# State-space outputs with the states as weights, and the mixer's branches in the other order, in a hybrid decoder block

## The chip, the core and the metric

The kernel runs on one core of a Trainium2 chip. The metric is the device time of one execution in microseconds (us), as the median over runs. TensorE (PE) multiplies; its weight loads are listed apart as PEld. VectorE (DVE), ScalarE (ACT) and GpSimd (POOL) work element by element, and SyncE (SP) issues most of the DMA transfers.

## The reference

One layer of a decoder block over 512 tokens of width 2048, in float32. What matters here is the first half, the mixer:

```python
h = modulate(rmsnorm(x, g_mix), shift1, scale1)          # shift, scale, gate: silu(c) @ w_ada
proj = h @ w_in + b_in                                   # -> q 1024, k 256, v 256, u 1024, gates 2 x 2048
q, k = rope_partial(q), rope_partial(k)
y_attn = sliding_window_attention(q, k, v, sinks) @ w_attn_branch       # window 128, 16 heads of 64
y_ssm = s5_ssm(u, ...) @ w_ssm_branch                    # 64 groups of 16 channels, 64 complex states each
merged = g[:, :, 0] * y_attn + g[:, :, 1] * y_ssm        # g = sigmoid(gate logits)
x = x + gate1 * (merged @ w_out)
# then the second half: x + gate2 * peer(h2, ...), a retrieval over 16384 experts, and a last rmsnorm
```

The state-space branch (`s5_ssm`) is linear in u: a recurrence x[t] = a x[t-1] + B u[t] with complex diagonal a, and y = Re(C x) + D u. Then z = gelu(y), and z * sigmoid(z @ w_glu + b_glu) is its output.

## The kernel before

Every matrix product with weights from memory is made exact enough by splitting: `weights` loads a tile of 1024 weights a row (`raw`), ACT rounds it to `whi` (L186), DVE forms the rest `wlo` (L188), and three matmuls per 128 x 128 block (L202, L203, L204) multiply the high and low parts of weights and activations. One such matmul is called dense below. A projection of 128 columns of `w_in` is 48 dense matmuls on 512 columns. The kernel is written in order, and a scheduler decides when it is built how the instructions of each engine follow one another; on the chip each engine takes its own in that fixed order and waits where an operand or a buffer is not there yet.

The mixer has these stages:

- **Head.** The columns of h become ready in five cuts (`HEAD_CUTS`), since each needs its part of `w_ada`, which DVE multiplies out (L141). `head_product` (L440 to L442) multiplies each cut with the u columns of `w_in` and accumulates eight PSUM tiles. In cuts 1 and 2, POOL makes `wlo` in place of DVE. Meanwhile POOL builds the constants of the recurrence; the largest are the rotations `rc` and `rs`, powers of a unit complex number for 64 chunks, made by six doublings (`cmul`, L343 to L348). They are written to memory as `rot_d` (L530, issued by SP). u goes to memory too (`u_d`).
- **State space with projections between.** The 512 steps are 64 chunks of 8. `ssm_slice` treats 4 pairs of groups; there are 8 slices. In a slice, (A) POOL multiplies out the matrices into and out of the chunks' states (`mt`, `cl_r`, `cl_i`); (B) PE turns `mt` (L582) and forms the kernel inside a chunk (`km`, L591, L592), which goes through memory (`km_d`, L599) and comes back spread out as `iraw` (L601), and u is loaded chunk by chunk (`uc`) and permuted (L614); (C) PE forms the inputs of the states (L624), and DVE rotates them, scans over the chunks and rotates back (L630 to L653), which gives the states `x_r`, `x_i`; (D) PE forms y: 24 matmuls, with `cl_r`, `cl_i` or `intra` as weights of 128 columns and the states or u as 64 moving columns (L662 to L664). y goes to `y_d` in pieces of 256 bytes. Buffers of a slice are mostly single. Between the parts of a slice stand projections, first k, v and q (with rotary embedding, `rope`), then gate logits (`sg_d`).
- **Attention with projections between.** 16 blocks (`attend`, a key-value head by 128 queries): scores (L700), softmax on DVE, ACT and POOL, transposes (L722), times v (L727). Between a block's scores and its transposes stands one projection. Then come 12 more projections.
- **Branch products.** y is loaded, passed through gelu (L763) and split, and then come `w_ab`, `w_glu`, `w_sb` and `w_out` with dense matmuls.

The second half (the retrieval) takes the rest and is the same in both kernels.

Of the kernel before, what the change touches and what calls it, by code (L numbers as in the profile page):

```python
# [19 lines left out]
T = 512  # L20
TT = 4
# [39 lines left out]
def hybrid_block(tc, I, out, dbg=None):  # L61
# [118 lines left out]
    loads = []  # L180

    def split_weights(src, part, sub=tt):
        r = wts.tile([128, 8, 128], F32, name="raw", tag="raw", bufs=4)[:, 0:part]
        loads.append(nc.sync.dma_start(r.rearrange("p a b -> p (a b)"), src).ins)
        h = wts.tile([128, 8, 128], F32R, name="whi", tag="whi")[:, 0:part]
        nc.scalar.copy(h, r)  # L186
        l = wts.tile([128, 8, 128], F32R, name="wlo", tag="wlo")[:, 0:part]
        sub(l, r, h.bitcast(F32), op=OP.subtract)  # L188
        return h, l
# [183 lines left out]
    nc.gpsimd.memset(rc[:, :, 0:1], 1.0)  # L373
    nc.gpsimd.memset(rs[:, :, 0:1], 0.0)
    w = 1
    while w < 64:
        ub, vb = (z[:, :, None].to_broadcast([128, PAIRS, w]) for z in (ur, ui))
        cmul(rc[:, :, w:2 * w], rs[:, :, w:2 * w], rc[:, :, 0:w], rs[:, :, 0:w], ub, vb, ra[:, :, 0:w])
        cmul(vr, vi, ur, ui, ur, ui, t0)
        ur, ui, vr, vi = vr, vi, ur, ui  # L380
        w *= 2
# [49 lines left out]
    def head_product(c):  # L431
# [27 lines left out]
    y_d = dr.tile([1024, 8, 64], F32, name="y_d")  # L459
# [8 lines left out]

    ap_ = pool("ap", "left")
    qr = ap_.tile([128, 8, T], F32, name="qr")  # L470
    kr = ap_.tile([128, 2, T], F32, name="kr")
    vv = ap_.tile([128, TT, 256], F32, name="vv")
    rp = pool("rp", "left")
    rcos = rp.tile([128, T], F32, name="rcos")
    rsin = rp.tile([128, T], F32, name="rsin")
    posi = tmp.tile([128, T], I32, name="t0", tag="t0")
    ang = row("ev")
    nc.sync.dma_start(posi, I["positions"][None, :].to_broadcast([128, T]))
    nc.vector.tensor_copy(ang, posi)
    ts(ang, ang, freq, None, op0=OP.mult)  # L480
    reduce_angle(ang, rcos)
    sin_cos(rsin, rcos, ang)
    ts(rsin, rsin, sgn, None, op0=OP.mult)
# [22 lines left out]
    def dense():  # L506
        jobs = [(8 + i, rope, kr[:, i]) for i in range(2)]
        jobs += [(10 + i, value, vv[:, :, i * 128:(i + 1) * 128]) for i in range(2)]
        jobs += [(i, rope, qr[:, i]) for i in range(8)]
        last = None  # L510
        for m, finish, dst in jobs:
            o = projected(m)
            if last:
                last[0](*last[1:])
            last = finish, dst, o
            yield
        for i in range(32):
            o = projected(20 + i, 1)
            nc.scalar.dma_start(sg_d[i], o)
            if last:  # L520
                last[0](*last[1:])
                last = None
            yield

    dense_work = dense()
# [10 lines left out]
    with tc.issue_after(loads[-1]):  # L536
        nc.sync.dma_start(bass.AP(tensor=km_d.tensor, offset=km_d[0].offset + 128, ap=[[240, 128], [30720, 8], [1, 112]]),
                            zero[:, None, :].to_broadcast([128, 8, 112]))
# [7 lines left out]
    def ssm_slice(s):  # L546
# [21 lines left out]
        cl_r, cl_i = tl("cl_r", [128, 4, 16, 8]), tl("cl_i", [128, 4, 16, 8])  # L568
# [9 lines left out]
        for mt, name in zip(mts, ("mi_r", "mi_i")):  # L578
            dst = tl(name, [128, 4, 128])
# [20 lines left out]
        iraw, intra = tl("iraw", [128, 8, 128]), tl("intra", [128, 8, 16, 8])  # L600
# [3 lines left out]
        rot = tl("rot", [128, 2, 256])  # L604
# [6 lines left out]
        u = tl("uc", [128, 8, 64])  # L611
# [3 lines left out]
        uj = tl("uj", [128, 8, 64])  # L615
# [12 lines left out]
        ta = tl("t2", [128, 512])[:, 0:256]  # L628
        w_r, w_i = (tl("mt", [128, 4, 16, 8], 2).rearrange("p a h j -> p (a h j)")[:, 0:256] for _ in range(2))
# [11 lines left out]
        x_r, x_i = tl("x_r", [128, 4, 64]), tl("x_i", [128, 4, 64])  # L641
# [25 lines left out]

    slices = [ssm_slice(s) for s in range(8)]
    next(slices[0])
    for s in range(8):  # L670
        for _ in slices[s]:
            next(dense_work)
        if s < 7:
            next(slices[s + 1])
    close(ss)
    close(sp)
    close(rp)
# [11 lines left out]
    def attend(b, n):  # L689
# [7 lines left out]
        for r2 in range(2):  # L697
            p = aux_tile().rearrange("p (a c) -> p a c", a=2)
            for r in range(2):
                nc.tensor.matmul(p[:, r, 0:wd], qr[rows, np_ * 4 + r2 * 2 + r, b * 128:(b + 1) * 128],  # L700
                                 kr[rows, np_, k0:k0 + wd], start=True, stop=True)
# [13 lines left out]
        yield  # L715
# [3 lines left out]
        for kc in range(nk):  # L719
# [3 lines left out]
            pt = aw.tile([128, 512], F32, name="pt", tag="pt", bufs=3)  # L723
# [7 lines left out]
    for b in range(TT):  # L731
        for n in range(4):
            for _ in attend(b, n):
                next(dense_work)
    close(aw)
    close(ap_)
# [23 lines left out]
    for k in range(8):  # L760
        y = row("ev")
        nc.sync.dma_start(y, y_d[k * 128:(k + 1) * 128].rearrange("p j c -> p (j c)"))
        act(z[:, k].rearrange("p (c j) -> p c j", j=8), y.rearrange("p (j c) -> p c j", j=8)[:, :, ::-1], AF.Gelu_apprx_tanh)  # L763
# [480 lines left out]

def shape_constants():
# [17 lines left out]
def device_inputs(x):  # L1263
# [5 lines left out]
    b_in = np.concatenate([l["b_in"][:1024][qo], l["b_in"][1024:]])  # L1269
    d = {  # L1270
# [8 lines left out]
                                                     l["b_glu"])], axis=1),  # L1279
# [3 lines left out]
        "w_sb": chunked(l["w_ssm_branch"]),  # L1283
        "w_glu": chunked(l["w_glu"]),
# [33 lines left out]
```

## Time and profile before

| | |
|---|---|
| time, median of 3 runs | 3734.87 us (3728.91 to 3746.68) |
| the profiled execution's own time | 3761.78 us |
| its span, first to last instruction | 3760.0 us |
| granted TensorE clock, mean | 0.961 of full speed |
| busy: PE, DVE, ACT, POOL | 94%, 71%, 34%, 24% |
| head, to the last L442 | to 208.4 us |
| state space with projections | 212.2 to 557 us |
| attention with projections, rest of the projections | 557 to 929 us |

PE is busy nearly always, but a matmul counts as busy from its start to its modelled end, and these overlap; how long a matmul really takes its place is the distance to the start of the next one. POOL and DVE count only while they compute.

### The profile page before, as it was taken

Reading aid. Unit: us, or ns where it says so; the run is one execution under the profiler, and the core shown is the slowest. Engines: PE = TensorE matmul, PEld = TensorE weight load, DVE = VectorE, ACT = ScalarE, POOL = GpSimd, SP = SyncE. Lnnn points to the kernel's source line nnn. Section 1 sums busy time; section 2 is a strip of 40 time slices with the busy share of each in tenths; the row PEclk is TensorE's granted clock in tenths of the full one; section 3 lists DMA queues with packets and bytes.
Section 4 is the critical chain, followed back from the end, with each engine's and each line's share of the span. In section 5 each row is a group of like instructions: output and inputs, shape, how many; then the busy total and the mean of one; then the engine's idle time right before and its main releaser. Section 6 shows DMA issues by size and latency. Waiting matters only on the chain.

```text
span 3760.0 us, 51345 instructions
## 1 busy us (share of the span) xinstructions
PE 3551.0 (94%) x20045; PEld 3227.8 (86%) x20045; DVE 2686.4 (71%) x4037; ACT 1291.9 (34%) x1788; POOL 906.7 (24%) x818
## 2 busy tenths in 40 slices
PE   7699999999999988999699999999999999999997
PEld 3477777777788888999699999999999999999997
DVE  7643545556874359989787788888888888877844
ACT  3232223333543342267232332233323323333333
POOL 7744530010000145310121222121221222222102
PEclk8888989999999999999899999999999999999998
DMA  8642445446964322266998898999999899978833
GB/s 287 210 156 79 126 135 179 171 159 251 335 215 167 119 88 69 86 218 241 322 351 303 329 340 338 334 334 340 347 334 344 328 335 346 342 274 310 321 128 112
DMA packets 274104, 921.60 MB, mean 245 GB/s; under 512 B 35394, under 2 KB 92866, under 8 KB 229956
## 3 DMA queue, kind: packets, MB, share of 16 engines
q1 hardware_dynamic: 204260, 533.91, 40.3%
q0 software_dynamic: 50048, 344.55, 24.9%
q10 hardware_dynamic: 19552, 39.85, 2.8%
q8 instruction: 157, 2.57, 0.3%
q14 instruction: 87, 0.71, 0.1%
HBM read 871.03 MB, written 47.12 MB: 244 GB/s over the span
## 4 chain that ended last, share of the span: by engine, by line
PE 76%; DVE 8%; DMA 7%; issue 2%; ACT 1%; POOL 1%; SPq 0%; DVEq 0%; ACTq 0%; POOLq 0%
PE mm L204 15%; PE mm L202 15%; PE mm L203 15%; PE aux L1200 8%; PE aux L1199 8%; PE aux L1198 8%; DMA gt<-g_d 3%; DMA raw<-in_up 2%; DVE wlo L188 1%; PE aux L1111 1%; DMA iraw<-km_d 1%; PE aux L664 1%; ACT whi L186 1%; PE aux L700 1%; PE aux L727 1%
## 5 line engine op out<-in xcount | busy, mean ns | idle before, releaser
L186 ACT CAST whi<-raw 128x1024 fp32r<-128x1024 f32 (+2 forms) x744 | 759.8, 1022 | 1687.3 <-PE mm L203 761.0
L188 DVE TENSOR_TENSOR wlo<-raw,whi 128x1024 fp32r<-128x1024 f32 (+2 forms) x696 | 851.6, 1224 | 424.9 <-ACT whi L186 400.8
L204 PE MATMUL mm<-h_hi,wlo 128*128 128x352 f32 (+1 forms) x2752 | 952.0, 346 | 10.4 <-DVE wlo L188 10.2
L202 PE MATMUL mm<-h_hi,whi 128*128 128x352 f32 (+1 forms) x2752 | 950.6, 345 | 5.7 <-ACT whi L186 5.7
L203 PE MATMUL mm<-h_lo,whi 128*128 128x352 f32 (+1 forms) x2752 | 947.7, 344 | 0.0
L1198 PE MATMUL aux<-wh,whi 128*128 128x352 f32 x2048 | 671.0, 328 | 50.0 <-ACT wh L192 26.9
L1200 PE MATMUL aux<-wh,wlo 128*128 128x352 f32 x2048 | 673.6, 330 | 25.5 <-DVE wlo L188 25.4
L1199 PE MATMUL aux<-wl,whi 128*128 128x352 f32 x2048 | 670.5, 327 | 2.3 <-DVE wl L193 2.3
L204 PEld LDWEIGHTS mm<-h_hi,wlo 128*128 128x128 f32 x2752 | 523.6, 190 | 44.0 <-DVE wlo L188 14.2
L202 PEld LDWEIGHTS mm<-h_hi,whi 128*128 128x128 f32 x2752 | 523.2, 190 | 37.7 <-ACT whi L186 6.7
L203 PEld LDWEIGHTS mm<-h_lo,whi 128*128 128x128 f32 x2752 | 524.8, 191 | 32.0 <-issue 4.4
L1198 PEld LDWEIGHTS aux<-wh,whi 128*128 128x128 f32 x2048 | 393.3, 192 | 56.8 <-ACT whi L186 29.7
L1200 PEld LDWEIGHTS aux<-wh,wlo 128*128 128x128 f32 x2048 | 392.9, 192 | 33.0 <-DVE wlo L188 32.7
L1199 PEld LDWEIGHTS aux<-wl,whi 128*128 128x128 f32 x2048 | 392.8, 192 | 3.3 <-DVE wl L193 3.3
L1028 DVE SCALAR_TENSOR_TENSOR rows<-rows,hrow 128x2048 f32<-128x2048 f32 x160 | 365.4, 2284 | 17.2 <-DMA rows<-in_down_rows,pick 16.9
L141 DVE SCALAR_TENSOR_TENSOR adaw<-adaw,cb 128x1024 f32<-128x1024 f32 x176 | 230.5, 1316 | 146.9 <-DMA adaw<-in_w_ada 146.7
L1022 POOL DMA_INDIRECT rows<-in_down_rows,pick x128 | 149.8, 1170 | 693.3 <-DVE rows L1028 390.3
L1039 DVE SCALAR_TENSOR_TENSOR yrow<-rows,fit,yrow 128x2048 f32<-128x2048 f32 x127 | 297.9, 2346 | 0.1
L1022 POOL DMA_INDIRECT rows<-in_up_rows,pick x128 | 146.0, 1140 | 560.1 <-DVE rows L1028 446.9
L1201 DVE SCALAR_TENSOR_TENSOR x<-aux,mod,x 128x352 f32<-128x352 f32 x256 | 148.4, 580 | 140.1 <-PE aux L1200 139.7
L214 POOL TENSOR_TENSOR rstd<-rstd,t 128x512 f32<-128x512 f32 (+2 forms) x42 | 52.8, 1258 | 610.9 <-ACT t L212 610.2
L188 POOL TENSOR_TENSOR wlo<-raw,whi 128x1024 fp32r<-128x1024 f32 (+1 forms) x48 | 104.7, 2188 | 101.1 <-ACT whi L186 99.8
(439 smaller groups left out, 4529.0 us busy)
## 6 DMA issues: line engine op xcount, KB each, us to landing
raw<-in_down SPq DMA_DIRECT2D x256, 512.0 KB
raw<-in_up SPq DMA_DIRECT2D x256, 512.0 KB
adaw<-in_w_ada SPq DMA_DIRECT2D x192, 512.0 KB
raw<-in_w_in SPq DMA_DIRECT2D x88, 512.0 KB
g_d<-stg ACTq DMA_DIRECT2D x22, 1024.0 KB
gt<-g_d SPq DMA_DIRECT2D x16, 1408.0 KB
raw<-in_w_out SPq DMA_DIRECT2D x32, 512.0 KB
raw<-in_w_query SPq DMA_DIRECT2D x32, 512.0 KB
```

The costliest lines, as they stand in the source:

```text
L141: stt(w, w, 1.0, cb[:, half], op0=OP.mult, op1=OP.mult, accum_out=part[:, half:half + 1])
L186: nc.scalar.copy(h, r)
L188: sub(l, r, h.bitcast(F32), op=OP.subtract)
L202: nc.tensor.matmul(p, h[:, k], (xh[kk] if isinstance(xh, list) else xh[:, kk]), start=first, stop=False)
L203: nc.tensor.matmul(p, h[:, k], (xl[kk] if isinstance(xl, list) else xl[:, kk]), start=False, stop=False)
L204: nc.tensor.matmul(p, l[:, k], (xh[kk] if isinstance(xh, list) else xh[:, kk]), start=False, stop=last)
L1022: nc.gpsimd.indirect_dma_start(out=r.rearrange("p k c -> p (k c)"), out_offset=None, in_=I[table], in_offset=bass.IndirectOffsetOnAxis(ap= ...
L1028: stt(r, r, 1.0, hrow, op0=OP.mult, op1=OP.mult, accum_out=f[:, n:n + 1])
L1039: stt(y, r, f[:, n:n + 1], y, op0=OP.mult, op1=OP.add)
L1198: nc.tensor.matmul(p, h[:, j], WH[j], start=(j == 0), stop=False)
L1199: nc.tensor.matmul(p, h[:, j], WL[j], start=False, stop=False)
L1200: nc.tensor.matmul(p, l[:, j], WH[j], start=False, stop=(j == GI - 1))
```

## The change

It has six parts. (1) The rotations are built by a function, `rotations`, that is called after the last POOL `wlo` of the head, and `rot_d` and the zeros in `km_d` are written from POOL's queue. (2) The state space comes directly after the head, with 16 gate logits between, and k, v, q come after it. (3) In `ssm_slice` most buffers are double, DVE's work has buffers of its own (`ta`, `w_r`, `w_i`), and the parts of neighbouring slices are written interleaved, so that part A runs two slices ahead. (4) y is formed with the states (or u) as weights of 64 columns and `cl_r`, `cl_i` or `intra` as 128 moving columns, and then turned by 16 matmuls of 64 x 64; the gelu is taken there (L651), and the result goes to memory in whole rows. The channels of the state-space branch have another order for that (`state_order`, on the host). (5) In the attention the scores of a block are formed before the projections that precede the transposes of the block before. All projections are used up there: 7 of the 12 for k, v and q stand ahead of it, and the other 5 and 16 gate logits inside. (6) z is loaded with the gelu already taken.

```diff
-    nc.gpsimd.memset(rc[:, :, 0:1], 1.0)
...
+    def rotations(ur, ui, vr, vi):
+        nc.gpsimd.memset(rc[:, :, 0:1], 1.0)
+        nc.gpsimd.memset(rs[:, :, 0:1], 0.0)
+        w = 1
+        while w < 64:
+            ub, vb = (z[:, :, None].to_broadcast([128, PAIRS, w]) for z in (ur, ui))
+            cmul(rc[:, :, w:2 * w], rs[:, :, w:2 * w], rc[:, :, 0:w], rs[:, :, 0:w], ub, vb, ra[:, :, 0:w])
+            cmul(vr, vi, ur, ui, ur, ui, t0)
+            ur, ui, vr, vi = vr, vi, ur, ui
+            w *= 2
+        for i, t_ in enumerate((rc, rs)):
+            nc.gpsimd.dma_start(rot_d[:, :, i], t_.rearrange("p (a b) c -> p a b c", a=8))
...
+            if c == 2 and i == 7:
+
+                with tc.issue_after(subs[-1]):
+                    rotations(ur, ui, vr, vi)
...
-    with tc.issue_after(loads[-1]):
-        for i, t_ in enumerate((rc, rs)):
-            nc.sync.dma_start(rot_d[:, :, i], t_.rearrange("p (a b) c -> p a b c", a=8))
...
+        p = aux_tile()
+        for a in range(4):
+            for n_ in range(3):
+                for two in range(2):
+                    rows = slice(two * 64, two * 64 + 64)
+                    o = p[rows, a * 128:(a + 1) * 128]
+                    if n_ < 2:
+                        x_, cl_ = ((x_r, cl_r), (x_i, cl_i))[n_]
+                        nc.tensor.matmul(o, x_[rows, a], cl_[rows, a].rearrange("p h j -> p (h j)"), start=(n_ == 0), stop=False)
+                    else:
+                        nc.tensor.matmul(o, uj[:, 2 * a + two], intra[:, 4 * two + a].rearrange("p h j -> p (h j)"),
+                                         start=False, stop=True)
+        y = tl("y", [128, 8, 64])
+        nc.scalar.copy(y, p.rearrange("p (m j) -> p j m", j=8))
+        p = aux_tile()
+        for j in range(8):
+            for two in range(2):
+                rows = slice(two * 64, two * 64 + 64)
+                nc.tensor.matmul(p[rows, j * 64:(j + 1) * 64], y[rows, j], ident[rows, rows], start=True, stop=True)
+        zs = tl("zs", [128, T])
+        act(zs.rearrange("p (c j) -> p c j", j=8), p.rearrange("p (j c) -> p c j", j=8)[:, :, ::-1], AF.Gelu_apprx_tanh)
+        nc.scalar.dma_start(y_d[s], zs)
...
+    for s in range(8):
+        next(slices[s])
+        next(dense_work)
+        if s < 7:
+            next(slices[s + 1])
+        next(slices[s], None)
+        if s < 6:
+            next(slices[s + 2])
+        next(dense_work)
...
-        y = tl("uc", [128, 8, 64])
-        for two in range(2):
-            p = aux_tile()
-            rows = slice(two * 64, two * 64 + 64)
-            for a in range(4):
-                g = 2 * a + two
-                o = p[:, a * 64:(a + 1) * 64]
-                nc.tensor.matmul(o, cl_r[rows, a].rearrange("p h j -> p (h j)"), x_r[rows, a], start=True, stop=False)
-                nc.tensor.matmul(o, cl_i[rows, a].rearrange("p h j -> p (h j)"), x_i[rows, a], start=False, stop=False)
-                nc.tensor.matmul(o, intra[:, 4 * two + a].rearrange("p h j -> p (h j)"), uj[:, g], start=False, stop=True)
-            nc.scalar.copy(y[:, two::2], p[:, 0:256].rearrange("p (a c) -> p a c", a=4))
-        nc.scalar.dma_start(chunked_ap(y_d), y)
...
+    blocks = [attend(b, n) for n in range(4) for b in range(TT)]
+    next(blocks[0])
+    for i, block in enumerate(blocks):
+        with tc.issue_after(next(blocks[i + 1])) if i + 1 < len(blocks) else contextlib.nullcontext():
+            for _ in range(2 if i < 5 else 1):
+                next(dense_work, None)
+        next(block, None)
```

The order of POOL's instructions at the end of the head, before the change (L343 to L348 are the rotations, L188 is `wlo` of the head's weights, L544 the first instruction that uses the memory which `rc` and `rs` had):

```order
L346 TENSOR_TENSOR rs<-rc,sn 128x32x32
L344 TENSOR_TENSOR pt_135<-sn 128x32
L346 TENSOR_TENSOR vi<-cs,sn 128x32
L345 TENSOR_TENSOR rc<-rc,ra 128x32x32
L188 TENSOR_TENSOR wlo<-raw,whi 128x512
L345 TENSOR_TENSOR vr<-vr,pt_135 128x32
L188 TENSOR_TENSOR wlo<-raw,whi 128x512
L347 TENSOR_TENSOR ra<-rs,cs 128x1024
L188 TENSOR_TENSOR wlo<-raw,whi 128x512 x13
L544 MEMSET bd_1533 128x128
```

The same place of POOL after the change (L375 and L376 begin the rotations, L385 writes them to memory):

```order
L348 TENSOR_TENSOR vi<-vi,pt_135 128x32
L188 TENSOR_TENSOR wlo<-raw,whi 128x512 x16
L375 MEMSET rc 128x32
L376 MEMSET rs 128x32
L343 TENSOR_TENSOR cs<-vr 128x32
...
L347 TENSOR_TENSOR ra<-rs,cs 128x1024
L385 DMA rot_d<-rc 1024x1x256
L348 TENSOR_TENSOR rs<-rs,ra 128x32x32
L385 DMA rot_d<-rs 1024x1x256
L520 MEMSET bd_1499 128x128
```

All 16 `wlo` now stand ahead of the rotations; between L343 and L347 here 68 more instructions of the rotations are left out, and the first use of their memory follows directly behind the second write.

PE's order where a slice forms y, before (slice 2, counted from 0; the 64 at the end are the moving columns):

```order
L662 MATMUL aux<-x_r,cl_r 128x64 x2
L202 MATMUL mm<-h_hi,whi 128x512
L203 MATMUL mm<-h_lo,whi 128x512
L204 MATMUL mm<-h_hi,wlo 128x512
...
L663 MATMUL aux<-x_i,cl_i 128x64
L664 MATMUL aux<-uj,intra 128x64
L662 MATMUL aux<-x_r,cl_r 128x64
...
L582 MATMUL aux<-cst,mt 128x128 x8
```

PE's order at the same place of a slice after the change (`y` is the copy of the first result; `cst` is the identity that turns it):

```order
L639 MATMUL aux<-cl_r,x_r 64x128 x2
L639 MATMUL aux<-cl_i,x_i 64x128 x2
L641 MATMUL aux<-intra,uj 64x128 x2
L203 MATMUL mm<-h_lo,whi 128x512
L204 MATMUL mm<-h_hi,wlo 128x512
...
L649 MATMUL aux<-cst,y 64x64 x16
L600 MATMUL aux<-uc,mi_r 64x64 x8
L600 MATMUL aux<-uc,mi_i 64x64 x8
L558 MATMUL aux<-cst,mt 128x128 x4
```

The two halves of the output rows are now formed in turn (x2), with 128 moving columns. Rows that repeat are left out. The 24 matmuls are followed by 22 dense ones, the 16 that turn, part C of the next slice and the `mt` of the slice after it. Up to the first of the 24 there are 274 dense matmuls of `w_in` (192 of them ahead of the first `mt`, L558, where there were 74), and then 273 from the first of the 24 of slice 0 to that of slice 5; before, each slice had some 90.

SP's order at the end of the head, before (the loads of 128x256 are the head's last weights, those of 128x1024 the first dense ones):

```order
L184 DMA raw<-in_w_in 128x256 x12
L530 DMA rot_d<-rc 1024x1x256
L184 DMA raw<-in_w_in 128x1024
L530 DMA rot_d<-rs 1024x1x256
L537 DMA km_d<-t_1528 128x8x112
L184 DMA raw<-in_w_in 128x1024 x23
```

The same place of SP after:

```order
L184 DMA raw<-in_w_in 128x256 x13
L184 DMA raw<-in_w_in 128x1024
L137 DMA adaw<-in_w_ada 128x1024
L184 DMA raw<-in_w_in 128x1024
L137 DMA adaw<-in_w_ada 128x1024
```

The writes of `rot_d` and of the zeros in `km_d` have left this queue, and every load of gate weights has one of `w_ada` behind it from the first on.

## Rows read from the trace of the kernel before

**Rows 1.** Windows: stretch, length, busy of PE PEld DVE ACT POOL, clock, DMA share, GB/s.

```profile
70.00:104.00 34.00, 28.55 (x100) 20.89 (x100) 31.72 (x58) 10.89 (x19) 33.77 (x44) 0.83 0.89 317
104.00:132.60 28.60, 0.36 (x2) 0.00 (x0) 7.05 (x13) 0.00 (x0) 28.60 (x37) 0.58 0.14 50
132.60:208.40 75.80, 70.39 (x284) 54.39 (x284) 52.91 (x80) 29.25 (x50) 29.64 (x20) 0.96 0.72 244
208.40:212.20 3.80, 1.48 (x5) 0.42 (x3) 1.23 (x1) 2.13 (x2) 0.00 (x0) 0.85 1.07 386
212.20:557.00 344.80, 338.81 (x1804) 268.23 (x1804) 161.92 (x288) 90.77 (x113) 170.23 (x186) 0.88 0.39 120
557.00:929.00 372.00, 372.00 (x1608) 284.55 (x1608) 208.66 (x329) 129.99 (x271) 31.05 (x16) 0.99 0.50 182
```

**Rows 2.** PE in order of time: start, us, what, [idle before <-releaser].

```profile
132.61 0.80 PE L442 MATMUL aux<-h_hi,wlo 128*128 128x512 f32 x1 [28.25 <-POOL wlo L188]
```

**Rows 3.** POOL in order of time, the head's end and the first slice.

```profile
69.68 0.24 POOL L343 TENSOR_TENSOR cs<-vr 128x32 f32<-128x32 f32 x1
...
74.51 1.33 POOL L343 TENSOR_TENSOR rc<-rc,vr 128x32 f32<-128x32 f32 x1
...
138.51 3.37 POOL L348 TENSOR_TENSOR rs<-rs,ra 128x1024 f32<-128x1024 f32 x1
...
179.71 2.17 POOL L188 TENSOR_TENSOR wlo<-raw,whi 128x512 fp32r<-128x512 f32 x1 [1.46 <-ACT whi L186]
213.36 0.35 POOL L544 MEMSET bd<- 128x128 f32 x2 [31.49 <-DMA rot_d<-rs]
...
224.12 1.35 POOL L566 TENSOR_TENSOR mt<-mt,t 128x512 f32<-128x512 f32 x1
```

**Rows 4.** Chain that ended last, 140 to 260 us: start, us, what.

```profile
149.78 0.23 PE aux L440
...
201.68 8.04 DMA raw<-in_w_in
...
245.19 7.35 DMA iraw<-km_d
```

**Rows 5.** PE in order of time, y of slice 4 (from 0) and behind it.

```profile
424.36 0.44 PE L662 MATMUL aux<-x_r,cl_r 64*128 64x64 f32 x4
...
427.04 0.43 PE L662 MATMUL aux<-x_r,cl_r 64*128 64x64 f32 x2
427.32 0.38 PE L663 MATMUL aux<-x_i,cl_i 64*128 64x64 f32 x2
427.63 0.43 PE L664 MATMUL aux<-uj,intra 128*128 128x64 f32 x2
427.99 0.43 PE L662 MATMUL aux<-x_r,cl_r 64*128 64x64 f32 x2
...
431.38 0.69 PE L662 MATMUL aux<-x_r,cl_r 64*128 64x64 f32 x2
...
433.04 0.69 PE L662 MATMUL aux<-x_r,cl_r 64*128 64x64 f32 x2
...
436.22 1.91 PE L582 MATMUL aux<-cst,mt 128*128 128x128 f32 x8
...
438.36 0.63 PE L203 MATMUL mm<-h_lo,whi 128*128 128x512 f32 x1
438.79 0.63 PE L204 MATMUL mm<-h_hi,wlo 128*128 128x512 f32 x1
```

**Rows 6.** PE in order of time, `km` and part C of the same slice.

```profile
406.25 0.36 PE L591 MATMUL aux<-cl_r,bd 128*32 128x112 f32 x2
406.45 0.35 PE L592 MATMUL aux<-cl_i,bd 128*32 128x112 f32 x2
...
409.78 0.69 PE L624 MATMUL aux<-uc,mi_r 128*64 128x64 f32 x16
410.39 0.50 PE L203 MATMUL mm<-h_lo,whi 128*128 128x512 f32 x1
```

More of the change, by code (lines that the diff above doesn't have):

```diff
@@ L504, in value, with gate_logits @@
         nc.scalar.copy(dst, p.rearrange("p (b c) -> p b c", b=TT))
[L506 to L517, printed above, removed]
+    def gate_logits(ids):
+        for i in ids:
             o = projected(20 + i, 1)
             nc.scalar.dma_start(sg_d[i], o)
-            if last:
-                last[0](*last[1:])
-                last = None
             yield
-    dense_work = dense()
-    with tc.issue_after(loads[-1]):
-        for i, t_ in enumerate((rc, rs)):
-            nc.sync.dma_start(rot_d[:, :, i], t_.rearrange("p (a b) c -> p a b c", a=8))
+    dense_work = gate_logits(range(16))
     close(st0)
@@ L535, in hybrid_block @@
     nc.gpsimd.memset(zero, 0.0)
-    with tc.issue_after(loads[-1]):
-        nc.sync.dma_start(bass.AP(tensor=km_d.tensor, offset=km_d[0].offset + 128, ap=[[240, 128], [30720, 8], [1, 112]]),
-                            zero[:, None, :].to_broadcast([128, 8, 112]))
+    nc.gpsimd.dma_start(bass.AP(tensor=km_d.tensor, offset=km_d[0].offset + 128, ap=[[240, 128], [30720, 8], [1, 112]]),
+                        zero[:, None, :].to_broadcast([128, 8, 112]))
     diag = ss.tile([32, 16], F32, name="diag")
@@ L626, in ssm_slice @@
             pv.append(p[:, 0:256])
-        ta = tl("t2", [128, 512])[:, 0:256]
-        w_r, w_i = (tl("mt", [128, 4, 16, 8], 2).rearrange("p a h j -> p (a h j)")[:, 0:256] for _ in range(2))
+        ta, w_r, w_i = (tl(n_, [128, 256]) for n_ in ("ta", "w_r", "w_i"))
         tt(w_r, pv[0], rcos_, op=OP.mult)
@@ L668, in hybrid_block @@
+        nc.scalar.dma_start(y_d[s], zs)
     slices = [ssm_slice(s) for s in range(8)]
-    next(slices[0])
+    for s, n in ((0, 2), (1, 1)):
+        for _ in range(n):
+            next(slices[s])
     for s in range(8):
-        for _ in slices[s]:
-            next(dense_work)
+        next(slices[s])
+        next(dense_work)
         if s < 7:
             next(slices[s + 1])
+        next(slices[s], None)
+        if s < 6:
+            next(slices[s + 2])
+        next(dense_work)
     close(ss)
@@ L676, in hybrid_block @@
     close(sp)
-    close(rp)
+    ap_ = pool("ap", "left")
+    qr = ap_.tile([128, 8, T], F32, name="qr")
+    kr = ap_.tile([128, 2, T], F32, name="kr")
+    vv = ap_.tile([128, TT, 256], F32, name="vv")
+    rp = pool("rp", "left")
+    rcos = rp.tile([128, T], F32, name="rcos")
+    rsin = rp.tile([128, T], F32, name="rsin")
+    posi = tmp.tile([128, T], I32, name="t0", tag="t0")
+    ang = row("ev")
+    nc.sync.dma_start(posi, I["positions"][None, :].to_broadcast([128, T]))
+    nc.vector.tensor_copy(ang, posi)
@@ new lines, in hybrid_block, with heads @@
+    ts(ang, ang, freq, None, op0=OP.mult)
+    reduce_angle(ang, rcos)
+    sin_cos(rsin, rcos, ang)
+    ts(rsin, rsin, sgn, None, op0=OP.mult)
+    jobs = [(8, rope, kr[:, 0]), (10, value, vv[:, :, 0:128])] + [(i, rope, qr[:, i]) for i in range(4)]
+    jobs += [(9, rope, kr[:, 1]), (11, value, vv[:, :, 128:256])] + [(i, rope, qr[:, i]) for i in range(4, 8)]
+    def heads():
+        last = None
+        for m, finish_, dst in jobs:
+            o = projected(m)
+            if last:
+                last[0](*last[1:])
+            last = finish_, dst, o
+            yield
+        gates = gate_logits(range(16, 32))
+        next(gates)
+        last[0](*last[1:])
+        yield
+        yield from gates
@@ L678, in hybrid_block @@
+    dense_work = heads()
+    for _ in range(7):
+        next(dense_work)
     if "q" in dbg:
@@ L699, in attend @@
             for r in range(2):
-                nc.tensor.matmul(p[:, r, 0:wd], qr[rows, np_ * 4 + r2 * 2 + r, b * 128:(b + 1) * 128],
-                                 kr[rows, np_, k0:k0 + wd], start=True, stop=True)
+                scored = nc.tensor.matmul(p[:, r, 0:wd], qr[rows, np_ * 4 + r2 * 2 + r, b * 128:(b + 1) * 128],
+                                          kr[rows, np_, k0:k0 + wd], start=True, stop=True).ins
             stt(sv[:, 2 * r2:2 * r2 + 2], p[:, :, 0:wd], 0.125, mk[:, None, :].to_broadcast([128, 2, wd]),
@@ L729, in attend @@
         split(hi, lo, po[rows].rearrange("p (r q) -> p r q", r=4))
[L731 to L734, printed above, removed]
+    blocks = [attend(b, n) for n in range(4) for b in range(TT)]
[5 more added lines that the diff above has]
+        next(block, None)
     close(aw)
+    close(rp)
     close(ap_)
```

60 lines of the change are left out of this document (19 added, 41 removed).

## The prediction

> **What bounds the kernel now.** I read the windows by stage first [rows 1]. PE is busy in nearly all of every stage but one: from 104.0 to 132.6 us it does 0.36 us of work, while POOL is busy for all 28.60 us and the DMA share is 0.14. In the order of time PE's next matmul names the reason: it waited 28.25 us for a `wlo` that POOL makes [rows 2]. That `wlo` stands behind POOL's rotations, which run from 74.51 to beyond 141 us [rows 3]. So POOL bounds the head, and PE the rest of the mixer. The state-space stage takes 344.8 us with PE busy 338.8 [rows 1]; there the question is what fills PE. A dense matmul takes a slot of 0.23 us [rows 4], and the granted clock is 0.88 of full speed in this stage, 0.99 in the attention [rows 1]. Where y is formed the rows show low clock: the same three matmuls take 0.95 us (427.04 to 427.99) and then 1.66 us (431.38 to 433.04), and behind them a dense one takes 0.43 us (438.36 to 438.79) [rows 5]. Attention is full: 372.00 of 372.00 us [rows 1]. The chain has two transfers that PE stood for [rows 4].
>
> **The head: -28 us.** With all 16 `wlo` ahead of the rotations, PE's wait of 28.25 us [rows 2] goes. POOL makes a `wlo` in about 1.3 to 2.2 us [rows 3], and what held it in the wait was the rotations alone, since it was busy for the whole stretch [rows 1]. What could be late next is the load of weights or DVE: transfers were nearly idle in the wait (0.14) because the buffers were full, and in the 75.8 us behind it had a share of 0.72, DVE 52.91 us of work [rows 1]; both still fit. Bounds: -20, if these catch up only in part, to -32.
>
> **First weights and first `iraw`: -7 us.** At the head's end PE is busy 1.48 of 3.80 us [rows 1], and the chain there is a load of weights of 8.04 us [rows 4], which SP issues around the write of `rot_d`. That write leaves SP's queue, so the load comes earlier: -3 or -4. The chain's 7.35 us for `iraw` [rows 4], of which about half is idle PE, is the second: with 274 dense matmuls ahead of the first y instead of 158 it should be covered, -3.5. Together -7, bounds 0 and -9.
>
> **The start of the slices: +13 us.** The rotations now begin behind the last `wlo`, which ended at 181.9 us [rows 3] and ends 28 us earlier, at 154. They took about 67 us, 5 of them for `wlo` between. They can take less: the same operation on 128x32 takes 0.24 us at 69.68 and 1.33 at 74.51 us [rows 3], where DVE was busy 31.72 of 34 us [rows 1]. I take 55 (45 to 62): they end at 209. The write of `rs` then holds POOL, since its first use of the memory stands right behind; I price the write like the 8.04 us of the load [rows 4], so POOL starts slice 0 at 217. From there to a first `mt` it took 12.1 us (213.36 to 225.5) [rows 3], thus 229. PE's head ends at 180.4, the first dense matmul follows at 182 at the latest, and 192 dense ones of 0.23 us stand ahead of the first turn of `mt`: 226. PE then waits 3 us, and again for the second `mt`, for `cl_i` and for `iraw`, each on POOL's way, some 10 more. POOL's wait for the write has the next slices' part A queued behind it. Bounds: 0 with rotations of 45 us, +25 with 62 and a slower write.
>
> **y: -45 us.** Now: slice 4's y lasts from 424.36 to 436.22, 11.9 us with six dense matmuls (1.4) between [rows 5], so 10.5, and 84 over eight slices. New: 24 matmuls of 128 columns and 16 of 64. No row shows these forms. Lower bound: the 16 records of part C, eight matmuls with 64 moving columns whose outputs are the two column halves, take 0.61 us (409.78 to 410.39) [rows 6], 0.076 each, thus 0.15 for 128 columns, 3.7 for 24, and 1.2 for the 16 that turn: 4.9 a slice, 39 in all, -45. Upper bound: a float32 matmul of 112 columns that overlaps nothing takes 0.20 us (406.25 to 406.45) [rows 6], so 0.23 for 128; 24 are 5.5, the changes between 64 and 128 rows add up to 0.6, the 16 that turn up to 2.1: 8.2 a slice, 66 in all, -18. I take the first, because output halves that alternate are what part C has. The copy on ACT and the gelu cost nothing: ACT is busy 90.77 of 344.8 us [rows 1], and the 22 dense matmuls (5 us) between the products and the turning cover the copy; without them PE would wait for about 2 us a slice.
>
> Three matmuls in a row started 0.28, 0.31 and 0.36 us after one another (427.04 to 427.99) [rows 5]: the larger ones are where the number of rows changes between 64 and 128, so a change costs 0.03 to 0.08 us. [...]
>
> **The clock: -12 us.** 0.12 of 344.8 us is 41 us lost to the low clock. Eight triples at 0.95 would be 7.6 us a slice, so 23 of it lies in y (84 less 61) and is counted above. The other 18 lie behind y, in the turn of `mt` at 436.22 and in dense matmuls at 0.43 us [rows 5]. The low clock always begins within the long row of matmuls with 64 columns; that row shrinks to about 4 us. I take two thirds, -12 (0 to -17).
>
> **The steady slices: +6 us.** From slice 0 to slice 5 there are 273 dense matmuls, 55 or 12.5 us a slice; with y 4.9 and the other small ones about 5.3 (part C 1.2 from its 0.61 [rows 6], `mt` 0.8 at full clock, `km` and the permutation 3.3 by slots like those of [rows 6]) PE needs 22.7 us. POOL computes 170.23 / 8 = 21.3 us a slice [rows 1], and waits for `km_d` besides. That is a tie where there was ample room (344.8 / 8 = 43 us a slice). I take 1 us for six slices, bounds 0 and +30 (5 us each).
>
> **The attention: +3 us.** Scores earlier give nothing where PE is never idle [rows 1]. With all projections used up inside, the last block has none behind its scores: one softmax is bare, 0 to +6. The second half is the same.
>
> **Sum.** -28 - 7 + 13 - 45 - 12 + 6 + 3 = -70. The profiled execution took 3761.78 us, so this makes 3692; it lies 27 us above the median of 3734.87, on which I put the same difference: **3665 us**. All bounds on the good side give -103 (3632), all on the bad side +23.
>
> **The rivals.** *The halves don't overlap* (chance 0.20): y costs 8.2 us a slice, the sum is -43, 3692. [...] *The start gives the head back* (0.20): rotations of 62 us or more beside a busy DVE, the start costs +25 and the clock gives nothing: -46, 3689. For it: 1.33 against 0.24 us [rows 3]. *The head's wait stays in the main* (0.10): the `wlo` wait for something else, the weights' load or `whi`, as the last one did for 1.46 us [rows 3], and the head gives 8 in place of 28: -50, 3685. Against it: POOL was busy throughout. *Slower* (0.05): the slice loop runs at the pace of POOL and the way `km`, `km_d`, `iraw`, which PE's 12.5 us of dense work a slice no longer covers. It decides where a slice takes 70 / 6 = 12 us more than 22.7, from about 35 us on; at 38 us the sum is +22, 3757. For it: POOL's 21.3 us lack all waits; against it: buffers are double and part A runs two slices ahead.
>
> **How the numbers follow.** The likeliest case has 0.45, its own range is 3645 to 3685. About 0.5% (18.7 us) is what a measurement of this kernel can tell from no change. The first three rivals are faster too, unless two of them and a slow steady slice meet; hence faster 0.88, same 0.07, slower 0.05. The range reaches from all bounds good, 3632, to the rivals with a slow steady slice on top, 3716.
>
> **What would show it.** In the trace of the changed kernel: no wait of more than 3 us for `wlo` in the head, and its last matmul near 180 us; the rotations' end between 199 and 216; PE's wait before the first turn of `mt`; y of a slice in 4 to 6 us; a granted clock of 0.93 or more in the state-space stage; slices about 23 us apart. Wrong it would be with slices 30 us apart, or with PE idle for more than 30 us between the head and the first y.

## The result and the profile after

The changed kernel takes 3718.1 us in the median of 20 runs, the kernel before 3745.8 in as many; the ratio is 0.9929, with an interval of 0.9916 to 0.9941. That is 28 us faster, where 70 were forecast, and 2 us outside the range, which ended at 3716. (The three runs that the prediction had to start from, 3734.87 us, lie 11 us under the median of twenty. From 3745.8 the same sum would have given 3676.) The profiled execution took 3716.06 us, near its median.

The windows by stage of the changed kernel, columns as in [rows 1]; the stages are the stretch in which PE had waited, the rest of the head, the slices, and the attention:

```profile
104.00:132.60 28.60, 20.90 (x82) 16.04 (x81) 27.96 (x44) 9.46 (x15) 11.33 (x7) 0.88 0.97 345
132.60:180.40 47.80, 41.50 (x167) 30.97 (x165) 33.47 (x53) 20.80 (x35) 41.63 (x68) 0.93 0.67 233
180.40:471.00 290.60, 261.62 (x1914) 200.00 (x1914) 184.85 (x278) 84.73 (x104) 195.52 (x200) 0.96 0.53 173
560.00:898.00 338.00, 322.69 (x1364) 238.96 (x1364) 185.31 (x305) 115.81 (x255) 27.68 (x16) 0.99 0.44 159
```

The empty stretch is gone, and the first product with the low part of a dense weight (L204) begins at 180.4 us instead of 212.2, as forecast. The granted clock in the slices is 0.96 in place of 0.88. But PE, which had been idle for 6 us in the slices and for none in the attention [rows 1], is now idle for 29.0 and 15.3 us. The form of y came out as forecast; PE in order of time, slice 2 of the changed kernel, a part of its y and the turn:

```profile
322.12 0.44 PE L639 MATMUL aux<-cl_r,x_r 64*64 64x128 f32 x4
322.39 0.39 PE L639 MATMUL aux<-cl_i,x_i 64*64 64x128 f32 x4
322.70 0.44 PE L641 MATMUL aux<-intra,uj 128*64 128x128 f32 x4
323.07 0.44 PE L639 MATMUL aux<-cl_r,x_r 64*64 64x128 f32 x4
...
330.19 1.15 PE L649 MATMUL aux<-cst,y 64*64 64x64 f32 x32
331.27 0.69 PE L600 MATMUL aux<-uc,mi_r 128*64 128x64 f32 x16
```

Six matmuls, two for each row, take 0.95 us (322.12 to 323.07), the time that three of the old form took (427.04 to 427.99 [rows 5]; the granted clock was 1.00 in both). A pair, one matmul for each half, thus takes 0.32 us, while a single one of 112 columns took 0.20 [rows 6]: the halves overlap, though not in full. Four such sixes and the turn (1.08 us) make 4.9 us a slice.

What PE waits for in the changed kernel, in the slices (180 to 471 us) and then in the attention (560 to 898 us): total, times, longest:

```profile
PE aux L558 <- ACT zs L651: 7.2, 4, 2.5
PE mm L204 <- DVE wlo L188: 5.7, 4, 2.7
PE aux L639 <- DVE x_r L625: 5.2, 3, 3.7
PE aux L641 <- ACT intra L579: 4.2, 1, 4.2
PE mm L202 <- ACT whi L186: 4.1, 2, 3.8
PE aux L567 <- POOL cl_r L549: 2.8, 1, 2.8
...
PE aux L756 <- ACT pt L753: 15.3, 12, 1.8
```

The last of them is the attention's whole idle time, at one place in twelve of its 16 blocks; PE in order of time:

```profile
737.17 1.03 PE L751 MATMUL aux<-cst,sc 128*128 128x128 f32 x8
739.42 1.07 PE L756 MATMUL aux<-pt,vv 128*64 128x512 f32 x2 [1.22 <-ACT pt L753]
```

The transposes now stand at the end of a projection, and the product with v right behind them, so that PE waits for ACT's copy of what it has just transposed. In the kernel before, 23 dense matmuls stood between the two. The largest in the slices, for `zs`, comes from an order too, that of ACT. ACT in order of time:

```profile
333.11 1.96 ACT L579 COPY intra<-iraw 128x1024 f32<-128x1024 f32 x1 [7.43 <-DMA iraw<-km_d]
334.98 1.04 ACT L186 CAST whi<-raw 128x1024 fp32r<-128x1024 f32 x1
335.92 0.59 ACT L651 ACTIVATE zs<-aux 128x512 f32<-128x512 f32 x1
```

ACT waits 7.43 us for the transfer of `iraw` of the next slice; the gelu (`zs`), whose operand PE had finished at about 331.3, stands behind that copy, and PE's turn of `mt` waits 2.48 us for the buffer that the gelu frees.

### The profile page after: what moved, and what is told of

It reads as the page before. It is cut to its first block, busy times and chain, and to the rows that moved or that the text cites. A ratio compares the mean times of both kernels' runs of the same rounds, so it can differ in the third digit from the quotient of the medians.

```text
span 3714.3 us, 51852 instructions
## 1 busy us (share of the span) xinstructions
PE 3497.6 (94%) x20301; PEld 3176.2 (86%) x20301; DVE 2718.3 (73%) x4037; ACT 1269.2 (34%) x1769; POOL 891.0 (24%) x821
## 4 chain that ended last, share of the span: by engine, by line
PE 71%; DVE 8%; DMA 5%; issue 2%; ACT 1%; POOL 1%; DVEq 0%; SPq 0%; ACTq 0%; POOLq 0%
PE mm L202 14%; PE mm L204 14%; PE mm L203 14%; PE aux L1232 8%; PE aux L1231 8%; PE aux L1230 8%; DMA gt<-g_d 2%; DVE wlo L188 1%; DMA raw<-in_up 1%; PE aux L1143 1%; PE aux L756 1%; PE aux L729 1%; ACT whi L186 1%; DMA rows<-in_down_rows,pick 1%; POOL wlo L188 0%
## 5 line engine op out<-in xcount | busy, mean ns | idle before, releaser
L188 DVE TENSOR_TENSOR wlo<-raw,whi 128x1024 fp32r<-128x1024 f32 (+2 forms) x696 | 856.9, 1232 | 411.3 <-ACT whi L186 363.4
L204 PE MATMUL mm<-h_hi,wlo 128*128 128x352 f32 (+1 forms) x2752 | 951.2, 346 | 15.1 <-DVE wlo L188 15.0
L204 PEld LDWEIGHTS mm<-h_hi,wlo 128*128 128x128 f32 x2752 | 521.0, 189 | 50.7 <-DVE wlo L188 20.2
L1054 POOL DMA_INDIRECT rows<-in_up_rows,pick x128 | 137.4, 1074 | 530.4 <-DVE rows L1060 416.9
L188 POOL TENSOR_TENSOR wlo<-raw,whi 128x1024 fp32r<-128x1024 f32 (+1 forms) x48 | 108.2, 2260 | 122.6 <-ACT whi L186 118.5
```

The lines of the kernel that those rows point to most:

```text
L188: subs.append(sub(l, r, h.bitcast(F32), op=OP.subtract).ins)
L204: nc.tensor.matmul(p, l[:, k], (xh[kk] if isinstance(xh, list) else xh[:, kk]), start=False, stop=last)
L1054: nc.gpsimd.indirect_dma_start(out=r.rearrange("p k c -> p (k c)"), out_offset=None, in_=I[table], in_offset=bass.IndirectOffsetOnAxis(ap= ...
```

## The experiments

Theory A: the terms for the head, y and the clock came in, and the rest was lost at places that the sum had at nothing or too low. Against it stand a smaller gain of y (B), POOL or the weights' loads as the bound (B and D), and, from the sixth run on, something behind the mixer (C, E). F and G, in the last four runs, are two ways in which that could come about.

**One part alone, on the kernel before; and one undone.** e1 puts the new y, its gelu and the order of channels into the kernel before (the copy y shares a buffer with `uc`, and `zs` one with `t0`, for want of space). e2 moves only the rotations. e3 changes only the attention's loop, and e4 mends that of the changed kernel:

```diff
         yield scored
-        po = aux_tile()
         nk = wd // 128
...
             pts.append(pt)
+        yield
+        po = aux_tile()
         for kc, pt in enumerate(pts):
...
         with tc.issue_after(next(blocks[i + 1])) if i + 1 < len(blocks) else contextlib.nullcontext():
+            next(block)
             for _ in range(2 if i < 5 else 1):
```

> The kernel before with only the new form of y (states as weights, turning, gelu at once, whole rows to memory). Theory A (the forecast's terms for y and the clock are right, and what is missing was lost elsewhere, in the attention and between the slices): y falls from 84 to about 40 us in the trace, the low clock behind it goes for the most part, 45 to 60 us faster than before. Theory B (the new form itself brings less than forecast): y alone still about 65 us or the low clock stays, under 30 us faster.

> The kernel before with only the rotations moved behind the last wlo of the head, written to memory from POOL's queue. Theory A: the head's wait of 28 us goes and at most 5 us of it come back at the first slice, 23 to 32 us faster. Theory B (the start of the slices gives the head back): the rotations end later than the dense work ahead of the first turn of mt can cover, under 15 us faster.

> The kernel before with only the scores of the attention one block ahead, blocks and projections otherwise in the order of before. In the built order the transposes now stand directly in front of the product with v, where 23 dense matmuls stood between. Theory A: PE waits some 1.4 us for the copy of the transposes in nearly each of 16 blocks, 14 to 22 us slower. Theory B (the waits in the attention come from what surrounds it, DVE or the loads): within 6 us of before.

> The changed kernel with the transposes of a block ahead of the projections and the product with v behind them. Theory A: the 12 waits of 15.3 us in all for the copy of the transposes go, and 12 to 18 us with them. Theory B (PE's waits only move to the next stage, because the loads of weights set the pace): within 6 us of the changed kernel.

| run | median, us | ratio to before (interval) |
|---|---|---|
| e1, new y alone | 3720.0 | 0.9931 (0.9905 to 0.9957) |
| e2, rotations alone | 3750.2 | 1.0012 (0.9994 to 1.0030) |
| e3, scores ahead alone | 3766.1 | 1.0061 (1.0038 to 1.0084) |
| e4, changed kernel, transposes early | 3699.2 | 0.9874 (0.9848 to 0.9901) |

e3 and e4 settle the attention: 21 us lost with the new order in the old kernel, 19 gained without it in the new one. In e3's trace PE waits 17.8 us for the copy of the transposes, in 14 blocks (the product with `w_out`, told of below, begins 30 us later in it, so its time also has other waits and a gain behind the mixer). In e4's trace PE is busy for 315.00 of 315.00 us from 560 to 875. But e1 and e2 gave less than theory A asked, though their traces agree with it. The product with `w_out`, the mixer's last, begins at these times (first and last start behind the durations) in the kernel before, in the changed kernel, in e1 and in e2:

```profile
L204 PE MATMUL mm<-m_hi,wlo x256: 392/392/394, 1154.2 to 1329.3; 128*128 128x512 f32 x128
```

```profile
L204 PE MATMUL mm<-m_hi,wlo x256: 392/392/394, 1118.4 to 1293.5; 128*128 128x512 f32 x128
```

```profile
L204 PE MATMUL mm<-m_hi,wlo x256: 392/392/394, 1112.9 to 1288.0; 128*128 128x512 f32 x128
```

```profile
L204 PE MATMUL mm<-m_hi,wlo x256: 392/392/394, 1145.6 to 1320.7; 128*128 128x512 f32 x128
```

So e1's mixer is 41 us shorter and e2's 9, and yet the medians say 25 shorter and 4 longer: in both some 15 us (16 and 13) went behind the mixer. e2 also shows what becomes of the head's 30 us in the old slices: all but 9 are gone by then. PE there waits for `whi` and `wlo` of the weights and for `intra` 20.6 us from 182 to 921 us (7.3, 7.1 and 6.2), where the kernel before has 6.0 from 212 to 929; that is 15 of the 21 us.

**The slices, and work added.** e5 holds the copy of `iraw` behind the gelu of the slice before; e7 moves five gate projections from the attention to the slices; e8 joins e4, e5 and e7. e6 adds dense matmuls behind the attention whose result is not used.

```diff
-        nc.scalar.copy(intra, iraw.rearrange("p g (j h) -> p g h j", h=16))
...
+        with tc.issue_after(turned[-1]) if turned else contextlib.nullcontext():
+            nc.scalar.copy(intra, iraw.rearrange("p g (j h) -> p g h j", h=16))
         pv = []
...
+    idle = aux_tile()
+    for i in range(176):
+        nc.tensor.matmul(idle, at_hi[:, 7, 0:128], at_hi[:, 7], start=(i == 0), stop=(i == 175))
+    nc.scalar.copy(row("t0"), idle)
```

> The changed kernel with the copy of iraw into intra put behind the gelu of the slice before, on ACT, instead of ahead of it. Theory A (ACT's fixed order gives the time of the transfer of iraw on to PE: gelu waits behind the copy, the turn of mt behind gelu): the waits of 7.2 us for zs before the turn of mt go, with the low clock that follows them 8 to 15 us. Theory B (POOL sets the pace of the slices): the waits move to mt or cl_r of POOL, within 5 us of the changed kernel.

> The changed kernel with 176 dense matmuls more between the attention and the branch products, whose result is not used: about 40 us of work on PE alone. In the traces so far, the part from the first matmul of the experts on (some 1940 us) seems 13 to 20 us longer where the mixer ends earlier than before. Theory A (what comes behind the mixer does not depend on when it starts): 38 to 42 us slower than the changed kernel. Theory C (a part of what the mixer gains is given back behind it, because something there does not start earlier): 20 to 30 us slower than the changed kernel.

> The changed kernel with five gate projections moved from the attention (one for each block there) to the slices, which thus have 21 in place of 16. Theory A and B alike: the slices from the third on have some 140 dense matmuls in place of 50, PE's waits between them (about 15 us from there on) go: 8 to 15 us faster than the changed kernel, less what the attention loses by thinner cover (its first five blocks wait as the others do, 1.4 us each, up to 7). Theory D (the loads of weights set the pace): no gain.

> The changed kernel with the transposes ahead of the projections, the copy of iraw behind the gelu, and 21 gates among the slices. Theory A: the gains add, 19 for the transposes and 12 to 25 for the others, 3675 to 3690 us. Theory B or D: no more than the transposes alone, about 3699 us.

e5 took 3714.7 us (0.9925, 0.9903 to 0.9947), e7 3721.9 (0.9945, 0.9926 to 0.9964): neither differs clearly from the changed kernel. In e5 the wait for `zs` is gone, but that for `x_r` grew from 5.2 to 11.0 us: a part of the wait moved on to the next in the slice's chain. The rest was gained, since `w_out` begins 10 us earlier (1108.7), within the 8 to 15 of theory A, and was lost again behind the mixer. e7's expectation failed: `w_out` begins 10 us later (1128.6), and PE waits 24.0 us for `whi` and `wlo` of the weights from 180 to 930 us, where the changed kernel has 9.8 in the lists above. That is what theory D asked for, but in e8, which has the same gates, the two are 7.5; why they are long in e7 stays open. e6 cost 25 us and not 40 (3743.4), as theory C has it, although `w_out` begins 46 us later. And e8 took 3666.8 us (0.9793, 0.9769 to 0.9817), less than the 3675 expected at best and 51 us less than the changed kernel, where the three parts alone had given 19, 3 and none. 37 of the 51 are the parts themselves, since `w_out` begins that much earlier in e8 (1081.8 against 1118.4). Some 15 us had come and gone again, as in e1, e2 and e6.

**The order at the program's end.** All kernels that had lost the 15 us shared one thing: the order of the experts' loads and products, which no edit touches, was another. It is decided when the program is built, and 8 matmuls added to the mixer turn it over (e9 below). SP's order where `x_d` is read back for the gathered rows, in the kernel before:

```
L184 DMA raw<-in_down 128x1024 x2
L1159 DMA rows<-x_d 128x16x128
L184 DMA raw<-in_down 128x1024 x11
```

and in the changed kernel:

```
L184 DMA raw<-in_up 128x1024 x13
L1191 DMA rows<-x_d 128x16x128
L184 DMA raw<-in_up 128x1024
L184 DMA raw<-in_down 128x1024 x12
```

At this place e3, e6 and e8 have the first order, e1, e2, e4, e5 and e7 the second. Four runs with 8 or 24 dense matmuls added to the kernel before, and 24 or 48 to the changed one, as in e6, turn the order or leave it:

> The kernel before with 8 dense matmuls more (1.8 us of PE) behind the attention, result unused. In the built order the loads and products of the experts at the end of the program then stand as they do in the changed kernel (SP reads x_d back between two loads of up weights), and not as in the kernel before (between two loads of down weights). Theory E (that order costs about 15 us, and every kernel that has it lost them): 12 to 22 us slower than before. Theory A (what comes behind the mixer is the same in both): 0 to 5 us slower.

> The kernel before with 24 dense matmuls more (5.5 us of PE) in the same place; the built order of the experts stays as it is in the kernel before. Both theories: 3 to 8 us slower than before; under theory E thus faster than with 8 matmuls more.

> The changed kernel with 24 dense matmuls more (5.5 us of PE); the order of the experts' loads stays as in the changed kernel. Both theories: 3 to 8 us slower than the changed kernel, about 3723 us.

> The changed kernel with 48 dense matmuls more (11 us of PE); the order of the experts' loads now is that of the kernel before. Theory E: 11 us more and about 15 less, 3 to 8 us faster than the changed kernel, about 3713 us. Theory A: 11 us slower than the changed kernel, about 3729 us.

| run | order at the end | median, us | ratio to before (interval) |
|---|---|---|---|
| e9, before + 8 | of the changed kernel | 3757.4 | 1.0039 (1.0019 to 1.0059) |
| e10, before + 24 | of before | 3741.8 | 0.9993 (0.9972 to 1.0013) |
| e11, changed + 24 | of the changed kernel | 3719.5 | 0.9925 (0.9902 to 0.9948) |
| e12, changed + 48 | of before | 3704.8 | 0.9902 (0.9867 to 0.9936) |

Theory E holds: 8 matmuls cost 15 us and 24 cost none (3 to 8 were expected); 48 make the changed kernel 13 us faster, more than the 3 to 8 expected. In e9 and e10 `w_out` begins at 1160.9 and 1160.7 us; the rest is the order. Behind it, what PE waits for in the experts' part, first e9 (from 1819 us), then e10 (from 1817 us):

```profile
PE aux L1204 <- DVE wlo L188: 33.5, 16, 7.8
PE aux L1202 <- ACT wh L192: 23.4, 1, 23.4
PE aux L1202 <- ACT whi L186: 13.1, 12, 5.1
PE mm L204 <- DVE wlo L188: 10.6, 5, 5.2
```

```profile
PE aux L1204 <- DVE wlo L188: 25.1, 15, 5.5
PE aux L1202 <- ACT wh L192: 23.2, 1, 23.2
PE aux L1202 <- ACT whi L186: 12.6, 12, 3.7
PE mm L204 <- DVE wlo L188: 4.5, 2, 4.0
```

The waits for `wlo` differ by 14.5 us. They part the other kernels too: in the experts' part PE waits 23 to 30 us for `wlo` in the six that have the order of the kernel before at `x_d` (29.9 in the kernel before), and 37 to 47 us in the eight that have the other (38.2 in the changed kernel). From the start of `w_out` to the end of the median run the six take 2575 to 2592 us and the eight 2593 to 2607. The kernel before is the longest of its six, at 2592; e6 and e10 take 2579 and 2581, and why it takes more is open.

DVE makes `wlo`, and stood for `gt`, the experts' gates, ahead of it: DVE's waits in the same stretches, e9 and then e10:

```profile
DVE a L1182 <- DMA gt<-g_d: 35.4, 9, 9.7
```

```profile
DVE a L1182 <- DMA gt<-g_d: 26.7, 9, 8.7
```

**By way of `gt`?** Four more runs take the loads of `gt` from SP's queue to POOL's, in the changed kernel (e13, e15) and in e8 (e14, e16); all of them in e13 and e14, all but the first in e15 and e16:

```diff
-        nc.sync.dma_start(gt, g_d[:, :, g * GI:(g + 1) * GI, :])
+        (nc.sync if g == 0 else nc.gpsimd).dma_start(gt, g_d[:, :, g * GI:(g + 1) * GI, :])
```

> The changed kernel with the loads of gt (the experts' gates, one of 1.4 MB for each group of experts) issued from POOL's queue, no longer between the loads of up weights on SP's. The order of the rest stays as in the changed kernel (x_d read back between two loads of up weights). Theory F (that order costs 15 us by way of gt: DVE waits for it 36 us in all, wlo stands behind on DVE, PE behind wlo): the waits for gt fall and 10 to 25 us go, 3693 to 3708 us. Theory G (the cost is in the places of the other instructions, x_d's read and what follows it on DVE and PE): within 6 us of the changed kernel.

> The version with all three edits (transposes early, iraw behind the gelu, 21 gates among the slices) and gt on POOL's queue. With gt there its built order is that of the changed kernel at x_d's read, where without it it was that of the kernel before. Theory F: 3645 to 3667 us, no slower than without. Theory G: about 15 us slower than without, 3677 to 3687 us.

> The changed kernel with the first load of gt on SP's queue as it is, and the others on POOL's. In the run with all of them on POOL's queue the first group of experts took 87 us in place of 70 and began 5 us later, and all further groups together 1841 in place of 1871 us. The order at x_d's read is now that of the kernel before. Theory F: the first group is back at 70 and the others keep their gain, 3685 to 3697 us. Theory G: the order alone brings its 15 us, 3700 to 3706 us.

> The version with all three edits and the same loads of gt; its order at x_d's read is that of the kernel before, as it was without this edit. Theory F: what SP's loads of gt cost in either order goes too (the groups behind the first took 1859 us without and 1845 us with all gt on POOL's queue), 3648 to 3658 us. Theory G: no change, 3662 to 3672 us.

e13 took 3711.9 us, e14 3673.1: between the theories (F: PE waits for `wlo` by way of `gt`; G: the places of the other instructions cost the time), since the first group of experts (from its first product to that of the next group) took 17 and 18 us longer, while the others together took 30 and 14 less. e15 took 3694.4 us (0.9852, 0.9825 to 0.9878), inside theory F's range, and e16 3657.8 (0.9764, 0.9736 to 0.9793), at the end of it. DVE's wait for `gt` falls from 36.0 us in the changed kernel to 7.1 in e13 and 3.0 in e15. But the way that theory F names is not what the traces show. PE's waits in the experts' part, in the changed kernel and then in e13:

```profile
PE aux L1232 <- DVE wlo L188: 34.0, 18, 9.1
PE aux L1230 <- ACT whi L186: 16.9, 17, 3.8
PE mm L204 <- DVE wlo L188: 4.2, 4, 1.6
```

```profile
PE aux L1232 <- DVE wlo L188: 44.0, 22, 6.4
PE mm L204 <- DVE wlo L188: 5.4, 2, 5.1
PE aux L1230 <- ACT whi L186: 4.2, 7, 0.8
```

Without the wait for `gt`, PE waits for `wlo` longer and not shorter, 49.4 us against 38.2; what falls is the wait for `whi`, from 16.9 to 4.2. In e15 the two are 35.4 and 5.8. And e8, which did not lose the 15 us, has 34.9 us of DVE's waits for `gt`. So e15 and e16 came into theory F's range by another way than F's, which is luck. They also have the order of the kernel before at `x_d`, so that they do not tell the load of `gt` from the order. That PE's waits for `wlo` go with the order is shown; how the order makes them is open. e16 is the fastest version of this study, 88 us faster than the kernel before.

## Why the prediction was wrong

- **The head, -28**, was right: the wait is gone and the dense products begin 31.8 us earlier (L204, 212.2 to 180.4), which takes in the first weights. **The start, +13**, was somewhat too high: PE waited about 8 us, 4 for POOL's `mt`, `cl_r` and `cl_i` up to the first y and 4.2 for `intra` within it. That last wait is the one for the first `iraw`, whose -3.5 thus did not come. The last `wlo` ended at 148.5 us and not 154, the rotations took 51.5 us and not 55, and POOL began the slices at 207.6 and not 217. Alone in the old kernel (e2) most of the head's gain is used up by other waits; the prediction gave that rival 0.20, and for the whole change it did not come.
- **y, -45**, was right: 4.9 us in slice 2, forecast 4.9. What the eight changes a slice between 64 and 128 rows cost lies within the spread of 0.27 to 0.37 us from one pair of y to the next (322.12, 322.39, 322.70 and 323.07).
- **The clock, -12**, came with the form of y and was for the most part given back. The windows from the first dense product (L204) to the first of `w_out`, columns as in [rows 1], in the kernel before, in the changed kernel, in e1 and in e8:

```profile
212.20:1154.20 942.00, 934.10 (x4373) 732.95 (x4374) 538.51 (x880) 330.88 (x518) 201.28 (x202) 0.95 0.52 179
180.40:1118.40 938.00, 891.43 (x4628) 685.93 (x4629) 566.19 (x878) 308.30 (x499) 223.20 (x216) 0.98 0.52 179
212.80:1112.90 900.10, 881.74 (x4628) 679.31 (x4629) 539.24 (x880) 311.18 (x499) 206.84 (x202) 0.99 0.55 187
181.30:1081.80 900.50, 879.75 (x4629) 681.32 (x4630) 557.68 (x878) 308.46 (x498) 228.48 (x216) 0.99 0.56 186
```

  PE's work in this stretch falls by 52 us in e1, of the 57 forecast for y and clock, and by 54 in e8. In the changed kernel it falls by 43 only. There the granted clock drops behind waits: in the slices it was below 1.00 in six stretches, each behind a wait of PE of 2.2 to 4.2 us. One of them, PE in order of time, and the window that follows:

```profile
291.63 0.44 PE L639 MATMUL aux<-cl_r,x_r 64*64 64x128 f32 x4 [3.72 <-DVE x_r L625]
...
293.42 0.63 PE L204 MATMUL mm<-h_hi,wlo 128*128 128x512 f32 x1
293.85 0.63 PE L202 MATMUL mm<-h_hi,whi 128*128 128x512 f32 x1
```

```profile
293.10:296.50 3.40, 3.40 (x10) 2.63 (x9) 0.92 (x3) 1.56 (x2) 3.16 (x5) 0.51 0.37 101
```

  A dense matmul takes 0.43 us there (293.42 to 293.85), where it takes 0.23 at a granted clock of 1.00 (318.06 to 318.29). The prediction priced the waits and the clock one by one; in this trace clock was lost behind the waits too.
- **The steady slices, +6**, is a step that failed. With the start (+13) and the first `iraw` (-3.5) some 15 us of idle PE were in the sum for the slices; the idle time grew by 23 (29.0 against 6.0). From the first y of slice 0 (256.46 us) to that of slice 5 (399.65) a slice takes 28.6 us, where the prediction had worked out 22.7 and named 30 as a sign of being wrong. It is no single bound: `zs`, `x_r`, `intra` and `whi` each end some of the waits, and in e5 a part of one wait, taken away, came back at the next.
- **The attention, +3**, is the other step of the mixer that failed: "one softmax is bare". PE waits 15.3 us there, and e3 and e4 put the whole at 19 to 21 us. The softmax was covered as forecast; what lay bare was the copy between the transposes and the product with v, since both had moved to the same end of a projection. The order that was at hand shows it, and the prediction did not look there.
- **"The second half is the same"** is the third: its code is, its order is not. The order costs 15 us in the old kernel (e9 against e10, `w_out` at the same time) and 25 in the changed one (e12 begins `w_out` 11.8 us later and is 13.3 us faster). Between these two kernels it cost less, about 8: `w_out` begins 35.8 us earlier, the median is 27.7 lower, and PE's waits for `wlo` in the experts' part are 8.3 us longer (38.2 against 29.9).

Together: behind the first dense product the sum had -38.5 up to `w_out`, and the windows above show -4 (942.0 to 938.0). PE is idle for 46.6 us of it in place of 7.9, which is 39 more, where the terms for waits (13, -3.5, 6 and 3) make 18.5: 20 of the 42 us that were missing are waits, 12 of them in the attention and 8 in the slices. Work that shrank by 43 and not by 57 is 14, most of it, by an estimate from the windows of e1 and e8 (52 and 54 at a granted clock of 0.99, where the changed kernel has 0.98), the low clock behind waits. The order of the experts is 8. Each start of `w_out` is from one profile, and such a start is known to some 5 us only (1118.4 in the changed kernel, 1117.4 and 1123.7 in e13 and e15, whose edits lie behind it).

## What to carry to other kernels

When a scheduler orders the program, compare its whole order with the one before, not only the part that was edited: a few microseconds upstream can turn over an order a millisecond later, and an edit is then judged with a loss or gain that is not its own. Work added that only shifts the time, at two or three sizes, tells the two apart. And when a stage is moved to cover one latency, look at each pair of dependent instructions on the busy engine for what now stands between them: the softmax was covered, the copy behind it lost its cover, 1.3 us in each of twelve blocks. What stands behind a wait for a transfer on an engine of fixed order (here the gelu behind `intra`, for which ACT waited 7.43 us) pays for that transfer too. A time that falls into the expected range does not show the way that was expected: in e13 to e15 the wait that theory F named was gone, and the wait that it should have shortened was not.

## What the runs showed of the hardware

Two matmuls of 64 output rows with 128 moving columns, in the two column halves, take 0.32 us together (0.95 us for six, 322.12 to 323.07), less than two single ones of 112 columns at 0.20 [rows 6]. With that form alone (e1) the granted clock in the slices was 0.98 (212.2 to 520 us) where it had been 0.88; in the changed kernel it was 0.96, and what low clock was left there stood behind waits of PE of 2.2 to 4.2 us (0.51 from 293.1 to 296.5, behind 3.72 us). POOL ran the rotations in less time behind its last `wlo` of the head than among the `wlo`, 51.5 us (148.5 to 200.0) against 67 (74.5 to 141.9), of which 5 were `wlo` and a wait for one. Loads of `gt` issued from POOL's queue cut DVE's waits for them from 36.0 to 7.1 us (e13), but the first group of experts then took 87 us in place of 70.
